# A third pair of output chunks by seven products, with tiles kept in DRAM meanwhile

## The chip, the cores and the metric

The kernel runs on one core of a Trainium2 chip. The time is that of the device in microseconds. A core has a matrix engine (TensorE, PE in the profile), a vector engine (VectorE, DVE), a scalar engine (ScalarE, ACT), GpSimd (POOL) and a queue engine (SyncE, SP). Each runs its own list of instructions in order, and waits on semaphores for the others. Sixteen DMA engines move data between DRAM and the on-chip memory (SBUF); here SP issues nearly all transfers, and GpSimd those that add to what lies in SBUF.

## What is computed

One layer of an encoder block, all in float32, 256 tokens by 2048 features:

```python
xn = rms_norm(x, norm_pre_w[l])
z = xn @ w_in[l]
u_lru, g_lru, q, k, v, g_attn, m_lru, m_attn = jnp.split(z, split_at, axis=-1)
u = centred_depthwise_conv(u_lru, conv_w[l], conv_b[l])
h = (rg_lru(u, ..., False) + rg_lru(u, ..., True))
y_a = h.astype(x.dtype) * jax.nn.silu(g_lru)
q = partial_rope(q.reshape(bsz, s, N_HEADS, HEAD_DIM), cos, sin)
k = partial_rope(k.reshape(bsz, s, N_KV_HEADS, HEAD_DIM), cos, sin)
v = v.reshape(bsz, s, N_KV_HEADS, HEAD_DIM)
y_b = windowed_gqa(q, k, v, attn_sink[l]) * jax.nn.silu(g_attn)
merged = (jax.nn.sigmoid(m_lru) * (y_a @ w_proj_a[l])
          + jax.nn.sigmoid(m_attn) * (y_b @ w_proj_b[l]))
x = x + rms_norm(merged @ w_out[l], norm_post_w[l])
```

`w_in` has 13312 columns: 2048 each for u, g_lru, q, g_attn, m_lru, m_attn, and 512 each for k and v. There are 16 heads of 128, and 4 of keys and values.

## The kernel before

**Products of float32 by three.** Every operand is split in a rounded part (`h`) and the rest (`l`), and a product is `h*h + h*l + l*h` (`mm3`, L151): three matmuls. ACT casts to `h`, DVE subtracts to get `l`.

**Steps and half steps.** The weights are read once, as rows of 1 MB (128 partitions by 2048 numbers). One row is one step of a list `steps`, and a step has two halves; the last loop of `body` (L887 to L904) walks over them. At half step `hs` it issues: the fetch of the row three steps ahead (SP, L142) into one of three buffers `raw`, whatever was put down for this half step with `at(hs, fn)` or `soon(fn, d)`, the cast and one half step later the subtraction of the half four ahead (`ahead` and `low`, L872 and L863, into one of five buffers each for `wh` and `wl`), and then the matmuls of the half. So each engine's order is written out by hand by these numbers, and the next fetch waits until DVE has subtracted both halves of an earlier row.

**Ways to make a chunk.** `add_rows` makes 512 output columns for both 128-token halves from four steps of 24 matmuls each. `add_pair` makes u and the two silu gates, features on partitions. `add_seven` (L533) makes two chunks of 512 columns at once as a 2 by 2 by 2 block product with seven block products in place of eight (`SEVEN`, L69); each takes two steps of 12 matmuls. Its left sides are blocks of the activations and four sums of blocks, e1 to e4 (`sums`, L589, which also splits them), and its right sides are weight blocks and running sums of them: those rows stay in one of two buffers `chain`, and GpSimd's DMA adds the next weight block to what lies there (L870). `spread` weaves the 14 steps of a seven among plain steps. Before the change there are two: chunks 1 and 2 of the lru merge gate (`ml`, among the gate pairs), and chunks 2 and 3 of `w_proj_a` (`pa`).

**Order.** u, ml chunk 0 and v; then the pairs for gl, ga and u with the ml seven and ml chunk 3 woven in, beside the recurrence (`lru_pair`, one every `LRU_PACE` half steps); then k; then q chunks 0 to 3 with the four chunks of the attention's merge gate (`ma`) among them as `FILL` says: q0, ma0, q1, ma1, q2, q3, ma2, ma3. Each q chunk starts four heads (`head`, L688), one every `HEADS_PACE` half steps, each a chain of PE, DVE and ACT pieces with fixed distances. After them come pa and pb, the merge, `w_out` and the tail.

**Memory.** Nearly all tiles (512 KB, that is 4 KB per partition) share `UNITS` = 31 places, and a place comes free when the last reader of its tile is done. Through the q chunks the kernel holds there the normalised x (`xn`, 8), silu(g_lru)*h = y (`sgl`, 4), the gate outputs `sga` (4), sigmoid(ml) (`tm`, 4), sigmoid(ma) (`sm`) and the attention's own tiles. The sums of x for the ml seven (`xe`) are made from half step `XE` = 36 on, at 36, 42, 48 and 54, and are dropped after it. PSUM has two double banks (`banks`) for accumulators of whole chunks, and four single ones (`bank`) for everything else.

Of the kernel before, what the change touches and what calls it, by code (L numbers as in the profile page):

```python
# [14 lines left out]
F32 = mybir.dt.float32  # L15
F32R = mybir.dt.float32r
# [4 lines left out]
P = 128  # L21
D = 2048
S = 256
# [10 lines left out]
LRU0 = 14  # L34
LRU_PACE = 18
XE = 36
XN = 15
HEAD0 = 5
HEADS_PACE = 3
FILL = ((0,), (1,), (), (2, 3))  # L40
YE = (8, 12, 18, 26)
FIRST = 8
ROWS = 10
# [31 lines left out]
def body(ctx, tc, x, xT, wall, wlru, pvec, npost, ident_d, mask_d, rope_d, out):  # L75
# [3 lines left out]
    chain = ctx.enter_context(tc.tile_pool(name="chain", bufs=CHAIN))  # L79
    ring = ctx.enter_context(tc.tile_pool(name="ring", bufs=3))  # L80
    small = ctx.enter_context(tc.tile_pool(name="small", bufs=2))
    psum = ctx.enter_context(tc.tile_pool(name="psum", bufs=4, space=PSUM))
    ctx.enter_context(tc.manual_schedule())

    def unit(name, dt=F32, shape=(P, 4, S)):
        return units.tile(list(shape), dt, tag="u", name=name)

    def bank(name, shape=(P, 2, S)):
        return psum.tile(list(shape), F32, tag="bg", name=name, bufs=4)

    def banks(name, shape=(P, 2, 2, S)):
        return psum.tile(list(shape), F32, tag="mm", name=name, bufs=2)
# [18 lines left out]
    def lag_parts(h, l, src):  # L111
        nc.scalar.copy(h, src)
        soon(lambda: nc.vector.tensor_tensor(l, src, h.bitcast(F32), ALU.subtract))

    rows_of = wall_rows()
    steps, due = [], {}
# [2 lines left out]
    def at(hs, fn):  # L119
        assert hs >= now[0], (hs, now[0])  # L120
        due.setdefault(hs, []).append(fn)
# [6 lines left out]
    def soon(fn, d=1):  # L128
        at(now[0] + d, fn)
# [57 lines left out]
    def add_rows(name, m, c, act, done, spare=False, last=False):  # L187


        got, held = [], []  # L190

        def products(t, g, h, wh, wl):
            ts = slice(t * P, (t + 1) * P)
            for j in range(2):
                k = 4 * g + 2 * h + j
                sl = slice(j * 512, (j + 1) * 512)
                a = act[k // 2][:, k % 2, :, ts]
                mm3(got[t], a[:, 0], a[:, 1], wh[:, sl], wl[:, sl], k == 0, k == KT - 1)

        def half(g, h, wh, wl):  # L200
            if g == 0 and h == 0:
                if spare:
                    got.extend(bank(f"{name}{t}", (P, 512)) for t in range(2))
                else:
                    ps = banks(name, (P, 2, 512))
                    got.extend(ps[:, t] for t in range(2))
            products(0, g, h, wh, wl)
            if last and g >= 2:
                held.append((1, g, h, wh, wl))
            else:  # L210
                products(1, g, h, wh, wl)
            if g == 3 and h == 1:
                if last:
                    done(0, got[0])
                    for a in held:
                        products(*a)
                    done(1, got[1])
                else:
                    soon(lambda: [done(t, got[t]) for t in range(2)])

        return [(("quad", m, c, g), lambda h, wh, wl, g=g: half(g, h, wh, wl), None) for g in range(4)]
# [284 lines left out]
    def gate_take(units_of, c, t, ps, scale=1.0):  # L506
        if c not in units_of:
            units_of[c] = unit(f"mg{c}", F32, (P, 2, 512))
        nc.scalar.activation(units_of[c][:, t], ps, AF.Sigmoid, scale=scale)

    def gate_evac(units_of, c, scaled=False):
        return lambda t, ps: gate_take(units_of, c, t, ps, rtok[:, t:t + 1] if scaled else 1.0)

# [72 lines left out]
                out.append((("quad", m, cols[c], 2 * r + i), lambda h, wh, wl, op=op, i=i: half(op, i, h, wh, wl), key and (name, key, i)))  # L586
        return out

    def sums(name, y):  # L589


        fm = lambda r, c, n: y[2 * c + n][:, :, r * P:(r + 1) * P]
        eight = lambda u: u.rearrange("p a (b c) -> p (a b) c", c=P)
        e, out = {}, {}

        def less(d, a, b):
            e[d] = e[b] if isinstance(b, str) else eight(unit(f"{name}{d}"))
            for n in range(2):
                f = [e[o][:, 4 * n:4 * n + 4] if isinstance(o, str) else fm(*o, n) for o in (a, b)]
                nc.vector.tensor_tensor(e[d][:, 4 * n:4 * n + 4], *f, ALU.subtract)  # L600

        def split_of(d):
            h, l = (unit(f"{name}{d}{s}", F32R, (P, 8, P)) for s in "hl")
            lag_parts(h, l, e[d])
            out[d] = (h, l)

        def when(hs):
            for (d, a, b), n in zip((("e1", (1, 0), (1, 1)), ("e2", (0, 0), "e1"), ("e4", (0, 1), "e2"), ("e3", (1, 0), (0, 0))), hs):
                at(n, lambda d=d, a=a, b=b: less(d, a, b))
                at(n + 2, lambda d=d: split_of(d))  # L610
            at(max(hs) + 4, e.clear)

        return out, when
# [10 lines left out]

        return left

    xe, xe_when = sums("xe", xt)
    xe_when([XE + n for n in (0, 6, 12, 18)])

    plain = []  # L630
# [12 lines left out]
    def add_heads(name, col, then):  # L643

        v = {}

        def evac(t, ps):
            if t == 0:
                v["t"] = unit(f"{name}t", F32, (P, 2, 512))
            nc.scalar.copy(v["t"][:, t], ps)  # L650
            if t == 1:
                soon(rotate)
                soon(flip, 3)
                for q in range(2):
                    soon(lambda q=q: part(q), 4 + q)

        def rotate():
            r = v["t"].rearrange("p t (h d) -> p t h d", h=4)
            both = small.tile([P, 2, 2, 4, ROT], F32, tag="lo", name=f"{name}r", bufs=1)
            c, m = both[:, 0], both[:, 1]  # L660
            table = lambda i, a, b: rope[:, :, i, a:b].unsqueeze(2).to_broadcast([P, 2, 4, b - a])
            half = ROT // 2
            nc.vector.tensor_tensor(m[:, :, :, 0:half], r[:, :, :, half:ROT], table(1, 0, half), ALU.mult)
            nc.vector.tensor_tensor(m[:, :, :, half:ROT], r[:, :, :, 0:half], table(1, half, ROT), ALU.mult)
            nc.vector.tensor_tensor(c, r[:, :, :, 0:ROT], table(0, 0, ROT), ALU.mult)
            nc.vector.tensor_tensor(r[:, :, :, 0:ROT], c, m, ALU.add)

        def flip():
            for q in range(2):
                v[q] = bank(f"{name}p{q}")  # L670
                for j in range(2):
                    n = 2 * q + j
                    for t in range(2):
                        nc.tensor.transpose(v[q][:, j, t * P:(t + 1) * P], v["t"][:, t, n * P:(n + 1) * P], ident)

        def part(q):
            if q == 0:
                v["h"], v["l"] = unit(f"{name}h", F32R), unit(f"{name}l", F32R)
            lag_parts(v["h"][:, 2 * q:2 * q + 2], v["l"][:, 2 * q:2 * q + 2], v[q])
            if q == 1:  # L680
                then(v["h"], v["l"])
                v.clear()

        return add_rows(f"{name}_", "w_in", col, xn, evac)
# [64 lines left out]
    def heads(g):  # L749
        def then(h, l):  # L750
            b = max(now[0] + HEAD0, ended[-1] if ended else 0)
            for j in range(4):
                head(4 * g + j, h, l, b + HEADS_PACE * j)
            ended.append(b + 4 * HEADS_PACE)
        return then
# [29 lines left out]
    def branch(name, m, y, take):  # L785
        pairs = {}

        def rows(q):
            a = pairs[q] = pair_unit(f"{name}y{q}")
            lag_parts(a[:, :, 0], a[:, :, 1], y[q // 2][:, q % 2 * 2:q % 2 * 2 + 2])  # L790

        def when(hs):
            for q in range(8):
                at(hs + q, lambda q=q: rows(q))

        def chunk(c):
            return add_rows(f"{name}{c}_", m, c * 512, pairs, lambda t, d: take(c, t, d))

        return pairs, when, chunk

    for i in range(4):
        steps += add_heads(f"q{i}", Q0 + i * 512, heads(i))
        for n in FILL[i]:
            steps += add_rows(f"ma{n}_", "w_in", MA0 + n * 512, xn, gate_evac(sm, n))
    pa, pa_when, pa_chunk = branch("pa", "w_proj_a", sgl, take_pa)
    pb, pb_when, pb_chunk = branch("pb", "w_proj_b", sga, take_pb)
    ye, ye_when = sums("ye", sgl)
    plain = [st for c in (0, 1) for st in pa_chunk(c)]
    b = 2 * len(steps)
    pb_first = pb_chunk(0)  # L810
    plain += pb_first + [st for c in (1, 2, 3) for st in pb_chunk(c)]
    pa_when(b - 4)
    ye_when([b + n for n in YE])
    steps += spread(plain, add_seven("pa", "w_proj_a", [3 * 512, 2 * 512], lefts(pa, ye), lambda t, j, d: take_pa(3 - j, t, d)), 2, 1.3)
    pb_when(2 * steps.index(pb_first[0]) - 4)
# [156 lines left out]
```

## Time and profile before

| | us |
|---|---|
| median of three runs | 904.03 (903.43 to 904.11) |
| the profiled execution | 904.01 |
| its span, first to last instruction | 902.2 |
| PE busy | 892.3 |
| DVE busy | 664.2 |
| ACT busy | 579.1 |

The mean granted TensorE clock was 0.997. In time order the stages are: u, ml0 and v to 78 us, the pairs with the recurrence and the ml seven to 403, k to 425, the q and ma chunks with the heads to 626, pa with its seven and pb to 805, and `w_out` with the tail to the end.

In the profile's rows a group reads: line of the kernel, engine, operation, tile written <- tiles read, shapes, count, then busy time and the mean of one in ns, then the time that the engine sat idle before them and what ended it. A row of a timeline begins with start and length in us. The row of a stretch gives its length and for each engine busy time and number of instructions, then the granted clock of TensorE, the share of the DMA engines and GB/s. In the list of DMAs the last number is the median time from issue to landing. `wh<-raw` is the cast of half a weight row, `wl<-raw,wh` the subtraction.

### The profile page before, as it was taken

Reading aid. Unit: us, or ns where it says so; the run is one execution under the profiler, and the core shown is the slowest. Engines: PE = TensorE matmul, PEld = TensorE weight load, DVE = VectorE, ACT = ScalarE, POOL = GpSimd, SP = SyncE. Lnnn points to the kernel's source line nnn. Section 1 sums busy time; section 2 is a strip of 40 time slices with the busy share of each in tenths; the row PEclk is TensorE's granted clock in tenths of the full one; section 3 lists DMA queues with packets and bytes.
Section 4 is the critical chain, followed back from the end, with each engine's and each line's share of the span. In section 5 each row is a group of like instructions: output and inputs, shape, how many; then the busy total and the mean of one; then the engine's idle time right before and its main releaser. Section 6 shows DMA issues by size and latency. Waiting matters only on the chain.

```text
span 902.2 us, 11861 instructions
## 1 busy us (share of the span) xinstructions
PE 892.3 (99%) x4590; PEld 763.9 (85%) x4590; DVE 664.2 (74%) x899; ACT 579.1 (64%) x807; POOL 14.6 (2%) x23
## 2 busy tenths in 40 slices
PE   9999999999999999999999999999999999999996
PEld 8888888888888888888888888888888888888885
DVE  6897989888787779696646757667888678655453
ACT  7968778786878686968455555467657555444441
POOL 0000000000000000000000000000000000000000
PEclk9999999999999999999999999999999999999998
DMA  8745686655486776545555445446757996568532
GB/s 328 259 150 216 247 278 196 229 197 232 187 237 206 234 210 199 198 168 201 184 185 173 162 144 179 147 176 242 168 205 239 243 246 196 196 218 295 189 137 94
DMA packets 29433, 184.78 MB, mean 205 GB/s; under 512 B 3264, under 2 KB 4160, under 8 KB 8768
## 3 DMA queue, kind: packets, MB, share of 16 engines
q1 hardware_dynamic: 26352, 166.08, 50.5%
q0 software_dynamic: 2304, 16.78, 10.1%
q10 hardware_dynamic: 720, 1.16, 0.4%
q8 instruction: 36, 0.59, 0.3%
q14 instruction: 21, 0.17, 0.1%
HBM read 181.90 MB, written 2.10 MB: 204 GB/s over the span
## 4 chain that ended last, share of the span: by engine, by line
PE 93%; DVE 3%; ACT 2%; DMA 1%; issue 1%; SPq 0%; DVEq 0%
PE ga L171 6%; PE gl L171 6%; PE u L171 4%; PE o L154 4%; PE o L152 4%; PE o L153 4%; PE ga L173 3%; PE gl L173 3%; PE u L173 2%; PE u_ps L354 2%; PE paq L548 2%; PE mlq L548 2%; PE pap L548 1%; PE mln L548 1%; PE pan L548 1%; PE gate L153 1%
## 5 line engine op out<-in xcount | busy, mean ns | idle before, releaser
L866 DVE TENSOR_TENSOR wl<-raw,wh 128x1024 fp32r<-128x1024 f32 x268 | 324.7, 1220 | 131.3 <-ACT wh L876 130.8
L876 ACT CAST wh<-raw 128x1024 fp32r<-128x1024 f32 x268 | 278.6, 1050 | 175.0 <-PE o L154 36.8
L876 ACT CAST wh<-chain 128x1024 fp32r<-128x1024 f32 x48 | 50.0, 1052 | 27.9 <-PE pb__6403 L154 5.0
L866 DVE TENSOR_TENSOR wl<-chain,wh 128x1024 fp32r<-128x1024 f32 x48 | 57.8, 1219 | 13.3 <-ACT wh L876 12.9
L171 PE MATMUL ga<-xn,wh 128*128 128x512 f32 x256 | 62.7, 391 | 0.0
L171 PE MATMUL gl<-xn,wh 128*128 128x512 f32 x256 | 62.7, 391 | 0.0
L171 PEld LDWEIGHTS gl<-xn,wh 128*128 128x128 f32 x256 | 47.0, 188 | 9.1
L171 PEld LDWEIGHTS ga<-xn,wh 128*128 128x128 f32 x256 | 46.9, 188 | 9.0
L152 PE MATMUL o<-wh,ms 128*128 128x512 f32 x128 | 49.9, 390 | 0.0
L154 PE MATMUL o<-wh,ms 128*128 128x512 f32 x128 | 49.8, 389 | 0.0
L153 PE MATMUL o<-wl,ms 128*128 128x512 f32 x128 | 49.8, 389 | 0.0
L171 PE MATMUL u<-xn,wh 128*128 128x512 f32 x192 | 47.4, 391 | 0.0
L171 PEld LDWEIGHTS u<-xn,wh 128*128 128x128 f32 x192 | 35.2, 188 | 6.8
L173 PEld LDWEIGHTS ga<-xn,wl 128*128 128x128 f32 x256 | 33.1, 191 | 1.4
L173 PEld LDWEIGHTS gl<-xn,wl 128*128 128x128 f32 x256 | 33.0, 191 | 1.2
L173 PE MATMUL ga<-xn,wl 128*128 128x256 f32 x256 | 33.9, 283 | 0.0
L173 PE MATMUL gl<-xn,wl 128*128 128x256 f32 x256 | 33.5, 283 | 0.0
L154 PEld LDWEIGHTS o<-wh,ms 128*128 128x128 f32 x128 | 24.0, 188 | 5.0
L153 PEld LDWEIGHTS o<-wl,ms 128*128 128x128 f32 x128 | 24.0, 188 | 5.0
L152 PEld LDWEIGHTS o<-wh,ms 128*128 128x128 f32 x128 | 24.0, 188 | 4.9
L870 POOL DMA_DIRECT2D chain<-wall_dram x16 | 14.1, 880 | 734.6 <-DVE wl L866 725.0
L173 PEld LDWEIGHTS u<-xn,wl 128*128 128x128 f32 x192 | 24.6, 191 | 0.9
(426 smaller groups left out, 2102.1 us busy)
## 6 DMA issues: line engine op xcount, KB each, us to landing
raw<-wall_dram SPq DMA_DIRECT2D x137, 1024.0 KB, 4.8
chain<-wall_dram POOLq DMA_DIRECT2D x16, 1024.0 KB, 8.1
chain<-wall_dram SPq DMA_DIRECT2D x8, 1024.0 KB, 7.0
lraw<-wlru_dram SPq DMA_DIRECT2D x8, 512.0 KB, 5.8
raw<-wall_dram SPq DMA_DIRECT2D x4, 512.0 KB, 7.2
xr<-x_dram SPq DMA_DIRECT2D x4, 512.0 KB, 9.7
raw<-wall_dram SPq DMA_DIRECT2D x4, 256.0 KB, 4.7
xT<-xT_dram SPq DMA_DIRECT2D x4, 256.0 KB, 6.5
```

The source lines that it names most:

```text
L152: nc.tensor.matmul(ps, wh, xh, start=start, stop=False)
L153: nc.tensor.matmul(ps, wh, xl, start=False, stop=False)
L154: nc.tensor.matmul(ps, wl, xh, start=False, stop=stop)
L171: nc.tensor.matmul(ps, wh[:, sl], a, start=k == 0, stop=k == KT - 1)
L173: nc.tensor.matmul(ps[:, 1], wl[:, sl], a[:, 0], start=False, stop=False)
L354: nc.tensor.matmul(ups[b // 2][:, b % 2, 0], w[:, sl], a[:, m], start=k == 0 and n == 0, stop=k == KT - 1 and n == 2)
L548: nc.tensor.matmul(d, x, y[:, sl], start=fresh and k == 0 and n == 0, stop=k == 7 and n == 2, skip_group_check=not fresh)
L866: nc.vector.tensor_tensor(wl, raws[i][:, h * 1024:(h + 1) * 1024], wh.bitcast(F32), ALU.subtract)
L870: nc.gpsimd.dma_start(raws[n], wall[rows_of[steps[n][0]]], accum_op=ALU.add)
L876: nc.scalar.copy(parts[q][0], raws[i][:, h * 1024:(h + 1) * 1024])
```

## The change

Chunks 0 and 1 of `ma` are now made by a seven, whose 14 steps are woven among the 24 steps of q0 to q3, ma2 and ma3 (`MA_SPREAD`: the first after one plain step, then one per 1.6). It needs the sums of x again. They are not made anew: when `sums` has split one, half steps later both parts are written to a DRAM pool `away` (`keep`), and read back some nine half steps before the product that takes them (`e_back`). To make room for them in the 31 places, sigmoid(ml) is written out at the end of the k chunk and read back when pa begins, and each quarter of y is written out when the recurrence has finished it and read back 14 half steps before pa begins. All these transfers are issued by SP in its order. Heads come every four half steps, not three, and the transposes of a q chunk go to one double bank, not to two single ones.

```diff
-HEADS_PACE = 3
-FILL = ((0,), (1,), (), (2, 3))
+HEADS_PACE = 4
+MA_SPREAD = (1, 1.6)
...
+    away = ctx.enter_context(tc.tile_pool(name="away", bufs=1, space=bass.MemoryType.DRAM))
...
+    def put_away(name, t):
+        d = away.tile(list(t.shape), F32, tag=name, name=f"{name}_away")
+        nc.sync.dma_start(d, t.bitcast(F32))
+        return d
+
+    def take_back(name, d, dt=F32, shape=(P, 4, S)):
+        t = unit(name, dt, shape)
+        nc.sync.dma_start(t.bitcast(F32), d)
+        return t
...
+    gone = {}
+
+    def gate_away(name, units_of, c):
+        gone[name, c] = put_away(f"{name}{c}", units_of.pop(c))
...
-    def sums(name, y):
+    def sums(name, y, keep=None):
...
+            if keep is not None:
+                soon(lambda: keep.update({d: [put_away(f"{name}{d}{s}", a) for a, s in ((h, "h"), (l, "l"))]}), 4)
...
-    xe, xe_when = sums("xe", xt)
+    kept = {}
+    xe, xe_when = sums("xe", xt, kept)
...
         def flip():
+            turned = banks(f"{name}p")
             for q in range(2):
-                v[q] = bank(f"{name}p{q}")
+                v[q] = turned[:, q]
...
+    b = 2 * len(steps)
+    for c in range(4):
+        at(b + c - 4, lambda c=c: gate_away("tm", tm, c))
+        at(LRU0 + LRU_PACE * (2 * c + 1) + 22, lambda c=c: gone.update({("ya", c): put_away(f"ya{c}", sgl[c])}))
+    plain = []
     for i in range(4):
-        steps += add_heads(f"q{i}", Q0 + i * 512, heads(i))
-        for n in FILL[i]:
-            steps += add_rows(f"ma{n}_", "w_in", MA0 + n * 512, xn, gate_evac(sm, n))
-    pa, pa_when, pa_chunk = branch("pa", "w_proj_a", sgl, take_pa)
+        plain += add_heads(f"q{i}", Q0 + i * 512, heads(i))
+    for n in (2, 3):
+        plain += add_rows(f"ma{n}_", "w_in", MA0 + n * 512, xn, gate_evac(sm, n))
+    me = {}
+    woven = add_seven("ma", "w_in", [MA0, MA0 + 512], lefts(xn, me), lambda t, j, d: gate_take(sm, j, t, d))
+    steps += spread(plain, woven, *MA_SPREAD)
+
+    def e_back(d):
+        me[d] = [take_back(f"me{d}{s}", a, F32R, (P, 8, P)) for a, s in zip(kept[d], "hl")]
+
+    for d, n in (("e1", 4), ("e4", 6), ("e3", 8), ("e2", 10)):
+        at(2 * steps.index(woven[n]) - 9, lambda d=d: e_back(d))
+    y_back = {}
+    pa, pa_when, pa_chunk = branch("pa", "w_proj_a", y_back, take_pa)
     pb, pb_when, pb_chunk = branch("pb", "w_proj_b", sga, take_pb)
-    ye, ye_when = sums("ye", sgl)
+    ye, ye_when = sums("ye", y_back)
...
     pa_when(b - 4)
+    for c in range(4):
+        at(b - 14 + c, lambda c=c: y_back.update({c: take_back(f"yb{c}", gone["ya", c])}))
+        at(b + c, lambda c=c: tm.update({c: take_back(f"tm{c}", gone["tm", c], F32, (P, 2, 512))}))
     ye_when([b + n for n in YE])
```

## The prediction

> **What bounds the kernel now.** I read the head of the page, then who TensorE waited for, then the stretches by stage, then single chunks in time.
>
> ```profile
> span 902.2 us, 11861 instructions
> PE 892.3 (99%) x4590; PEld 763.9 (85%) x4590; DVE 664.2 (74%) x899; ACT 579.1 (64%) x807; POOL 14.6 (2%) x23
> PE 93%; DVE 3%; ACT 2%; DMA 1%; issue 1%; SPq 0%; DVEq 0%
> ```
> ```profile
> PE spin L234 <- POOL eps L229: 1.0, 1, 1.0
> PE u_ps L354 <- ACT wh L105: 0.7, 1, 0.7
> ```
>
> The reader is to see that TensorE (PE) is busy for 892.3 of 902.2 us, that the chain that ended last is 93% PE, and that the whole list of PE's waits has two entries, 1.7 us together, both in the first microseconds. From there to the last chunk PE does not stop for anyone. The span is 902.2 us; the profiled execution took 904.01, so 1.81 lie around the span. That execution stands 0.02 under the median of three runs, 904.03, and I make the sum against it.
>
> ```profile
> core 0: us, PE busy (x) PEld busy (x) DVE busy (x) ACT busy (x) POOL busy (x), PEclk, DMA share, GB/s
> 78.00:180.00 102.00, 101.89 (x590) 89.94 (x589) 87.76 (x105) 80.61 (x111) 1.88 (x2) 1.00 0.68 232
> 290.00:403.00 113.00, 113.00 (x637) 99.27 (x636) 93.34 (x112) 84.96 (x114) 2.61 (x3) 1.00 0.63 198
> 425.00:640.00 215.00, 215.00 (x1067) 181.28 (x1066) 141.20 (x262) 121.79 (x194) 0.88 (x1) 1.00 0.50 175
> 640.00:700.00 60.00, 60.00 (x288) 50.29 (x288) 52.77 (x76) 39.24 (x53) 1.73 (x2) 1.00 0.68 219
> 700.00:765.00 65.00, 65.00 (x297) 53.99 (x296) 47.99 (x51) 34.62 (x37) 4.36 (x5) 1.00 0.84 226
> ```
>
> The stage that changes is that of the q chunks, the ma chunks and the heads; I take 425 to 640 for it, the first heads' half steps of pa included. There VectorE (DVE) works 141.2 of 215 us (66%), ScalarE (ACT) 121.8 (57%), the DMA engines half the time. The two stages that already hold seven-product pairs (180 to 403, and 640 to 780) run DVE at 83% (93.34 of 113) and 88% (52.77 of 60) and the DMA share up to 0.84, and PE is still full.
>
> **The change part by part.** First the matmuls. A chunk in rows has 4 steps of 24 matmuls of 512 columns, so two chunks have 192. Seven products have 14 steps of 12, which is 168. So 24 matmuls go.
>
> ```profile
> 424.96 0.39 PE L152 MATMUL q__4053<-wh,xn 128*128 128x512 f32 x1
> 433.29 0.87 PE kp L674 x8
> 447.62 0.39 PE L152 MATMUL ma__4221<-wh,xn 128*128 128x512 f32 x1
> 626.15 0.48 PE L152 MATMUL pa__5777<-wh,pay 128*128 128x512 f32 x1
> 683.94 2.72 PE paq L548 x12
> ```
>
> Chunk q0 begins at 424.96 and the next one at 447.62: 22.66 us, less 0.87 for the eight transposes put between, is 21.79 for 96 matmuls, 0.227 us each (the 0.39 of a row is one matmul's own length; they overlap). A step of seven products takes 2.72 us for 12, the same 0.227. So PE loses 24 x 0.227 = **5.44 us** of work. Heads, q transposes and all else on PE keep their count.
>
> What this costs on the other engines: 14 steps in place of 8 are 6 more, 12 halves, each with a cast on ACT and a subtraction on DVE.
>
> ```profile
> L866 DVE TENSOR_TENSOR wl<-raw,wh 128x1024 fp32r<-128x1024 f32 x66 | 80.4, 1222 | 38.9 <-ACT wh L876 38.9
> L876 ACT CAST wh<-raw 128x1024 fp32r<-128x1024 f32 x66 | 69.5, 1052 | 64.4 <-PE ma__4221 L154 10.6 <-PE q__4053 L154 9.0 <-PE q__4382 L154 8.6
> L574 DVE TENSOR_TENSOR pat<-pan,pat 128x512 f32<-128x512 f32 x1 | 0.7, 680 | 0.0
> L569 ACT COPY pat<-paq 128x512 f32<-128x512 f32 x1 | 0.6, 589 | 0.3 <-PE paq L548 0.3
> L712 ACT ACT_TABLE_LOAD x4 | 5.1, 1283 | 0.1
> ```
>
> DVE: 12 x 1.22 + 5 sums of 0.68 (L571 to L579) = 18.0, so 159.2 in about 209.6 us, 76%. ACT: 12 x 1.05 + 3 copies of 0.59 + one more pair of table loads of 1.28 (the ma sigmoids now fall in five places, not four) = 17.0, so 138.8, 66%. Both stay under the 83% and 75% of 290 to 403, so PE's work hides them, and I cost them at nothing. If that cover were gone, DVE's 18.0 would be the most that could appear.
>
> Heads three or four half steps apart: the pace is counted in half steps, and those get shorter (64 of them took 201 us, from 424.96 to the first pa matmul at 626.15, 3.14 each with the heads' matmuls among them; 76 will take some 195.8, 2.58 each). Four of the new are 10.3 us, three of the old 9.4. So a head gets about the time that it had, and the last one ends 16 half steps into the next stage (17 before). The q transposes go from two single banks of psum to one double, where accumulators change over once per chunk; a seven takes one of the four single banks through the whole stage, and a head at most three. I cost this at nothing, between a gain of 0.5 (the few short stalls now beside the transposes) and a loss of 0.5.
>
> Now SP's queue and the DMAs. Added are 16 writes of 512 KB (ml gates, y, and eight parts of the x sums) and 16 reads, 16.8 MB, and 6 more weight steps. The trace shows no write of that size, so I bound it:
>
> ```profile
> raw<-wall_dram SPq DMA_DIRECT2D x137, 1024.0 KB, 4.8
> chain<-wall_dram POOLq DMA_DIRECT2D x16, 1024.0 KB, 8.1
> chain<-wall_dram SPq DMA_DIRECT2D x8, 1024.0 KB, 7.0
> out_dram<-yw SPq DMA_DIRECT2D x4, 256.0 KB, 2.1
> GB/s 328 259 150 216 247 278 196 229 197 232 187 237 206 234 210 199 198 168 201 184 185 173 162 144 179 147 176 242 168 205 239 243 246 196 196 218 295 189 137 94
> ```
>
> A chain load is mostly issued right behind a raw load and lands 2.2 us later than one alone (7.0 against 4.8); at the fastest slice, 328 GB/s, 1.05 MB take 3.2 us. So what a transfer ahead costs the one behind it is 2.2 to 3.2 us per MB; I take 3.2. Among the q chunks this is hidden: there are 30 plain loads, 8 accumulating ones and some 7 MB more, and the stage 700 to 765 with DMA share 0.84 shows the worst of such traffic with PE full. In it PE still had the weights in hand:
>
> ```profile
> 698.65 1.22 DVE L866 TENSOR_TENSOR wl<-raw,wh 128x1024 fp32r<-128x1024 f32 x1
> 702.82 0.39 PE L152 MATMUL pb__6403<-wh,pby 128*128 128x512 f32 x1
> SPq L142 <- DVE wl L866: 669.3, 120, 12.6
> SPq L406 <- PE mlq L548: 3.8, 1, 3.8
> ```
>
> Counting halves in order, that subtraction (ends 699.87) feeds the half at 702.82: 2.95 us of lead, the shortest of that stage. Of the added waits, what is queued behind each on SP is the next weight fetch; but SP stands idle for 5.6 us per fetch anyway (669.3 in 120), waiting for the raw buffer. The writes come two or three half steps after their data, so they are ready about when SP gets there; the reads need a free place among the 31 units, and a load has already waited 3.8 us once for one (L406) with no stop on PE. Between 0 and 3.8 per read group, I take 0.
>
> The one place without cover is earlier, where the x sums are made and first written out (half steps 42 to 60, about 120 to 175 us):
>
> ```profile
> L113 DVE TENSOR_TENSOR xee2l<-xee,xee2h x1: 1220/1220/1220, 137.7 to 137.7; 128x1024 fp32r<-128x1024 f32 x1
> 155.83 1.22 DVE L113 TENSOR_TENSOR xee4l<-xee,xee4h 128x1024 fp32r<-128x1024 f32 x1
> 156.96 1.22 DVE L866 TENSOR_TENSOR wl<-raw,wh 128x1024 fp32r<-128x1024 f32 x1
> 159.42 1.22 DVE L866 TENSOR_TENSOR wl<-raw,wh 128x1024 fp32r<-128x1024 f32 x1
> ...
> 162.29 1.21 DVE L866 TENSOR_TENSOR wl<-raw,wh 128x1024 fp32r<-128x1024 f32 x1
> 163.62 0.39 PE L548 MATMUL mlp<-wh,xn 128*128 128x512 f32 x1
> 153.18 1.05 ACT L876 CAST wh<-raw 128x1024 fp32r<-128x1024 f32 x1
> 159.09 2.03 ACT L876 CAST wh<-raw 128x1024 fp32r<-128x1024 f32 x2 [1.58 <-DMA raw<-wall_dram]
> ```
>
> Here DVE runs almost without a break, and the subtraction that ends at 163.50 feeds the matmul at 163.62: 0.1 us of lead. The e2 parts (1.05 MB) are ready and written at about 139 (137.7 + 1.22); e4 (ready at 157.05) and the first y, 1.57 MB, go out at about 161, behind the fetch that waits for the subtraction of 159.42. What saves it is that DVE, not the fetch, is late: the cast of 153.18 ended at 154.23 and its subtraction came at 156.96, 2.7 us later; the pair cast from 159.09 has 2.1 us (160.14 to 162.29). The e2 writes can push the fetch between by about 2 of their 3.2; e4's writes sit behind the fetch that is needed next, and the lead after 170 grows again. So 0 to 3.2 us; I take **0.3**, near the covered end. The other writes meet leads of several us.
>
> Sum: 904.01 - 5.44 + 0.3 = **898.9 us**.
>
> **The rivals.** (1) Part is given back: one 1.05 MB write goes uncovered at the leadless place, 3.2 us: 904.01 - 5.44 + 3.2 = 901.8. For it: the 0.1 us of lead. Against: the 2.1 to 2.7 us between cast and subtraction.
> (2) Slower: there the fetches fall behind both groups of writes, 2.62 MB x 3.2 = 8.4 us, and nothing covers it, because a late cast makes a late subtraction, which frees the raw buffer late: 904.01 - 5.44 + 8.4 = 907.0. It decides once the fetches there are held up by more than 7.2 us beyond the casts' cover (5.44 are gained, 1.8 are the margin below). Against: the writes come two fetches apart, and the fetch behind the cast of 159.09 is issued between them. [...]
> (3) No change: PE's busy time isn't what sets the end, some other pace is, and the 24 matmuls leave as much idle time: 904.0. For it: the weight loads (PEld) fill 85%, not 99%. Against: the 0.227 us between matmuls is the same in a chunk of rows and in a seven, and no wait is on record. [...]
>
> **How the numbers follow.** A difference of 0.2%, 1.8 us, is about what a measurement of this kernel tells from none: faster is below 902.2, slower above 905.8. Forecast (898.2 to 900.4): 0.76. Rival 1 (900.4 to 903.5): 0.13, of which 0.08 below 902.2. Rival 2: 0.06. Rival 3: 0.05. Faster 0.84, same 0.10, slower 0.06. The range goes from 898.2 (5.44 and the 0.5 of the transposes, less 0.1) to 902.2, which leaves out about 0.17.
>
> **What would show it.** Right: PE busy near 887 us with 24 matmuls fewer, waits of PE still only those of the start, the q stage some 5.4 us shorter, DVE there at 76%. Wrong: PE waits on wl, wh, gate or sc; a PE busy sum that falls while the span doesn't (rival 3); between 150 and 175 us casts that wait for raw, and gl, mlp or gate behind them (rivals 1 and 2); fetches held on SP by a write's or a read's wait among the q chunks.

## The result, and the profile after

The changed kernel takes 899.19 us (median of six runs, 898.61 to 899.94), the kernel before 904.07 in the same comparison: a ratio of 0.9947, with a 95% interval from 0.9934 to 0.9960. A second comparison on another occasion gave 899.61 against 903.78, 0.9953 (0.9940 to 0.9965). The profiled execution took 899.15, its span is 897.0. The forecast was 898.9.

The head of the page after, and who TensorE waited for:

```profile
span 897.0 us, 11941 instructions
PE 885.6 (99%) x4566; PEld 759.1 (85%) x4566; DVE 680.5 (76%) x916; ACT 596.5 (67%) x824; POOL 21.5 (2%) x31
```
```profile
PE u_ps L365 <- ACT wh L106: 1.4, 1, 1.4
PE spin L245 <- POOL eps L240: 1.0, 1, 1.0
PE gate L163 <- ACT gi L458: 0.9, 1, 0.9
```

PE has 24 instructions fewer (4566, not 4590) and is busy 6.7 us less, the span is 5.2 us shorter. Two of the three waits are those of the first microseconds, as before. The third is new: a gate matmul of the recurrence waits 0.9 us for ACT. So some of the gain was lost in a stage that the seven doesn't touch.

The stretches (length; busy time and count by engine; granted clock; DMA share; GB/s), cut where the stages lie now:

```profile
79.00:181.00 102.00, 100.95 (x586) 89.12 (x585) 86.92 (x104) 78.44 (x107) 1.87 (x2) 1.00 0.77 269
426.00:635.00 209.00, 209.00 (x1049) 177.38 (x1048) 158.72 (x287) 138.48 (x212) 7.82 (x9) 1.00 0.76 243
```

Among the q chunks DVE now works 158.72 of 209 us (76%) and ACT 138.48 (66%), the DMA share rose from 0.50 to 0.76, and PE is full without a gap. Beside the recurrence PE is busy for 100.95 of 102 us, where it was 101.89.

Where the time went shows best from the starts of the first matmuls of each stage in the timelines. This table is worked out from those starts, in us:

| from, to | before | after | difference |
|---|---|---|---|
| span's start to the first gl matmul | 77.35 | 77.36 | +0.01 |
| first gl to first k matmul (the recurrence beside) | 325.82 | 326.88 | +1.05 |
| first k to first q matmul | 21.79 | 21.79 | 0 |
| first q to first `w_out` matmul | 381.17 | 375.19 | -5.99 |
| first `w_out` matmul to the last | 87.71 | 87.71 | 0 |
| last matmul to the span's end | 8.39 | 8.10 | -0.30 |
| around the span | 1.81 | 2.15 | +0.34 |

The rows that bound the fourth line, of before (its first row stands in the prediction) and of after:

```profile
806.14 0.39 PE L152 MATMUL o<-wh,ms 128*128 128x512 f32 x1
```
```profile
426.03 0.39 PE L163 MATMUL q__4086<-wh,xn 128*128 128x512 f32 x1
...
801.22 0.39 PE L163 MATMUL o<-wh,ms 128*128 128x512 f32 x1
```

So two things want a reason: the 5.99, which is 0.55 more than the 5.44 of the matmuls, and the 1.05 that came in earlier. The table has one more use. In the two profiles of the changed kernel the start of the first gl matmul moved by 0.65 us (77.36 and 78.01), while the stages behind it repeat within 0.1: differences of a few tenths are read from the stages, not from the whole times.

### Where the 1.05 us came from

SP's queue of the changed kernel, then the landing times of what it issued from 160.6 to 162.5, and the landing time of the same fetch in the kernel before:

```profile
160.68 0.33 SPq L153 DMA_DIRECT2D raw<-wall_dram  x1
161.06 0.43 SPq L118 DMA_DIRECT2D ya_away<-sg  x1
161.53 0.42 SPq L118 DMA_DIRECT2D xee4h_away<-xee4h  x1
162.00 0.89 SPq L118 DMA_DIRECT2D xee4l_away<-xee4l  x1
```
```profile
raw<-wall_dram SPq DMA_DIRECT2D x1, 1024.0 KB, 6.5
ya_away<-sg SPq DMA_DIRECT2D x1, 512.0 KB, 7.4
xee4h_away<-xee4h SPq DMA_DIRECT2D x1, 512.0 KB, 8.5
xee4l_away<-xee4l SPq DMA_DIRECT2D x1, 512.0 KB, 9.1
```
```profile
raw<-wall_dram SPq DMA_DIRECT2D x1, 1024.0 KB, 4.8
```

The fetch stands ahead of three writes, and yet lands 6.5 us after its issue in place of 4.8. What hangs on it is on ACT, here with PE's next gate matmul, first of before and then of after:

```profile
166.18 2.00 ACT L876 CAST wh<-raw 128x1024 fp32r<-128x1024 f32 x2
168.08 0.47 ACT L446 ACTIVATE gr<-gate,pv 128x256 f32<-128x256 f32 x1
168.45 0.47 ACT L447 ACTIVATE gi<-gate,pv 128x256 f32<-128x256 f32 x1
```
```profile
168.97 0.39 PE L152 MATMUL gate<-uh,lwh 128*128 128x256 f32 x1
```
```profile
167.22 2.00 ACT L914 CAST wh<-raw 128x1024 fp32r<-128x1024 f32 x2 [0.93 <-DMA raw<-wall_dram]
169.12 0.46 ACT L457 ACTIVATE gr<-gate,pv 128x256 f32<-128x256 f32 x1
169.49 0.46 ACT L458 ACTIVATE gi<-gate,pv 128x256 f32<-128x256 f32 x1
```
```profile
168.78 0.28 PE L165 MATMUL gate<-uh,lwl 128*128 128x256 f32 x1
170.00 0.39 PE L163 MATMUL gate<-uh,lwh 128*128 128x256 f32 x1 [0.95 <-ACT gi L458]
```

The reader is to see a chain through an engine's order. The casts wait for the fetch and run 1.04 us later (167.22 for 166.18). The sigmoids that read the gates' psum banks stand behind them in ACT's list, though they need nothing of that fetch. PE's next gate matmuls need those banks, and PE waits 0.95 us. Before, this place already had no time to spare: the gate matmul of 168.97 starts 0.05 us after the sigmoid that ends at 168.92. After, it starts at 170.00, again 0.05 after its sigmoid (169.95). The weights themselves were not late for PE: counted in order, the two subtractions of that row start at 170.39 and 171.52, as before (170.38 and 171.51), and end 6.4 to 6.6 us ahead of the matmuls that read them.

### The profile page after: what moved, and what is told of

The parts are those of the page before. It is cut to its first block, busy times and chain, and to the rows that moved or that the text cites. A ratio compares the mean times of both kernels' runs of the same rounds, so it can differ in the third digit from the quotient of the medians.

```text
span 897.0 us, 11941 instructions
## 1 busy us (share of the span) xinstructions
PE 885.6 (99%) x4566; PEld 759.1 (85%) x4566; DVE 680.5 (76%) x916; ACT 596.5 (67%) x824; POOL 21.5 (2%) x31
## 4 chain that ended last, share of the span: by engine, by line
PE 92%; ACT 2%; DVE 2%; DMA 2%; issue 1%; SPq 0%; DVEq 0%
PE ga L182 6%; PE gl L182 6%; PE u L182 4%; PE o L165 4%; PE o L164 4%; PE o L163 4%; PE ga L184 3%; PE gl L184 3%; PE u L184 2%; PE u_ps L365 2%; PE maq L564 2%; PE mlq L564 2%; PE paq L564 2%; DMA raw<-wall_dram 1%; PE man L564 1%; PE mln L564 1%
## 5 line engine op out<-in xcount | busy, mean ns | idle before, releaser
L904 DVE TENSOR_TENSOR wl<-raw,wh 128x1024 fp32r<-128x1024 f32 x256 | 309.9, 1220 | 106.0 <-ACT wh L914 105.2
L914 ACT CAST wh<-raw 128x1024 fp32r<-128x1024 f32 x256 | 266.0, 1051 | 165.4 <-PE o L165 36.8
L914 ACT CAST wh<-chain 128x1024 fp32r<-128x1024 f32 x72 | 75.0, 1051 | 39.7 <-PE pb__6724 L165 5.0
L904 DVE TENSOR_TENSOR wl<-chain,wh 128x1024 fp32r<-128x1024 f32 x72 | 86.9, 1220 | 16.2 <-ACT wh L914 15.4
L908 POOL DMA_DIRECT2D chain<-wall_dram x24 | 21.0, 877 | 722.7 <-DVE wl L904 711.0
```

The costliest lines, as they stand in the source:

```text
L904: nc.vector.tensor_tensor(wl, raws[i][:, h * 1024:(h + 1) * 1024], wh.bitcast(F32), ALU.subtract)
L908: nc.gpsimd.dma_start(raws[n], wall[rows_of[steps[n][0]]], accum_op=ALU.add)
L914: nc.scalar.copy(parts[q][0], raws[i][:, h * 1024:(h + 1) * 1024])
```

## The experiments

Eight runs follow, seven of them of kernels with an edit. The theory: PE's count of matmuls makes the gain, and the writes at 161 us cost the 1 us. The rivals: the new order, pace and banks make the gain; the 1 us is something else.

### The changed kernel once more

> The changed kernel again, beside the others on one chip. Expected as measured: about 899.2 us, span near 897.0, one new wait of PE of some 0.9 us (a gate matmul near 170 us, behind ACT's sigmoids).

It took 899.61 us (five runs), span 897.6, with the same wait of 0.9 us at the gate. The recurrence's stage was 326.81 us, the stretch from q to `w_out` 375.19, both within 0.1 of the first profile; the 0.6 us of the span lie in its start.

### The two chunks in rows again, all transfers kept

```diff
-HEADS_PACE = 4
+HEADS_PACE = 3
...
+    b = len(steps)
     for i in range(4):
-        plain += add_heads(f"q{i}", Q0 + i * 512, heads(i))
-    for n in (2, 3):
-        plain += add_rows(f"ma{n}_", "w_in", MA0 + n * 512, xn, gate_evac(sm, n))
+        steps += add_heads(f"q{i}", Q0 + i * 512, heads(i))
+        for n in ((0,), (1,), (), (2, 3))[i]:
+            steps += add_rows(f"ma{n}_", "w_in", MA0 + n * 512, xn, gate_evac(sm, n))
...
-    woven = add_seven("ma", "w_in", [MA0, MA0 + 512], lefts(xn, me), lambda t, j, d: gate_take(sm, j, t, d))
-    steps += spread(plain, woven, *MA_SPREAD)
...
-    for d, n in (("e1", 4), ("e4", 6), ("e3", 8), ("e2", 10)):
-        at(2 * steps.index(woven[n]) - 9, lambda d=d: e_back(d))
+    for d, n in (("e1", 11), ("e4", 16), ("e3", 21), ("e2", 27)):
+        at(2 * (b + n) - 9, lambda d=d: e_back(d))
```

> The changed kernel with ma chunks 0 and 1 made in rows again (192 matmuls in place of 168), in the old order and with heads every three half steps; all writes to DRAM and reads back stay, though the sums read back feed nothing. Theory (PE's count of matmuls sets the time, the writes beside the recurrence cost about 1.1 us): some 1 us slower than the kernel before, 904.9 to 905.5, PE's wait at the gate near 170 us still there. Rival (the gain comes from the new order, pace and banks and not from the count; the transfers are free): not slower than the kernel before, 903.5 to 904.3, no wait at the gate.

It took 904.76 us against 903.78: a ratio of 1.0011 (1.0002 to 1.0020). The theory had asked for 904.9 to 905.5, so the time lies 0.14 under its range. The difference of 0.98 is the 1 us that it asked for, and the sign is the theory's: without the seven, the change is slower. PE's waits:

```profile
PE spin L245 <- POOL eps L240: 1.0, 1, 1.0
PE gate L163 <- ACT gi L458: 0.9, 1, 0.9
PE u_ps L365 <- ACT wh L106: 0.2, 1, 0.2
```

The wait at the gate is there. The recurrence's stage is 327.23 us, 0.35 longer than the changed kernel's. The matmul starts show where: a matmul of the ml seven at 208.2 us starts right behind the subtraction that it reads, 0.05 us after it, and some 0.4 us are lost there. In the kernel before the same matmul had 1.5 us in hand, in the changed kernel 0.3. The three fetches that the changed kernel issues from 166.5 to 172.8 us land after 6.9, 8.6 and 7.5 us, those of the kernel before after 4.7, 4.9 and 5.8; the subtraction starts 2.26 us later than before (207.07 for 204.81), the matmul only 1.04. So the late fetches eat up the lead of a second place, which the changed kernel just clears.

```profile
206.96 1.22 DVE L902 TENSOR_TENSOR wl<-chain,wh 128x1024 fp32r<-128x1024 f32 x1
...
208.23 0.50 PE L564 MATMUL mlq<-wl,xee1h 128*128 128x512 f32 x1
```

And the stretch from q to `w_out`:

```profile
425.80 0.39 PE L163 MATMUL q__4085<-wh,xn 128*128 128x512 f32 x1
...
806.98 0.39 PE L163 MATMUL o<-wh,ms 128*128 128x512 f32 x1
```

It is 381.17 us, as in the kernel before. So the reads back, at the places that they have here, the late writes and the q transposes in a double bank cost PE nothing there, and the whole of the 5.99 belongs to the seven, with its order of the chunks, and the heads' pace. This run undoes these together; the pace alone is the fifth experiment.

### The early writes put off

```diff
+LATER = {"e1": 40, "e2": 36, "e4": 44, "e3": 40}
...
-... for a, s in ((h, "h"), (l, "l"))]}), 4)
+... for a, s in ((h, "h"), (l, "l"))]}), LATER[d])
...
-        at(LRU0 + LRU_PACE * (2 * c + 1) + 22, lambda c=c: gone.update(...))
+        at(max(98, LRU0 + LRU_PACE * (2 * c + 1) + 22), lambda c=c: gone.update(...))
```

> The changed kernel with the writes of the x sums put off by 32 to 40 half steps (half steps 78 to 96) and the first y's write to 98, where PE has its weights 4 us or more ahead. Theory (the writes near 161 us share the DMA engines with the weight fetch, its cast comes late, the sigmoids and the gate matmul behind it): the fetch issued near 160.7 lands by 165.6 again, PE's wait at the gate goes, span 895.7 to 896.3, time 1 us under the changed kernel, 897.9 to 898.4. Rival (the 1 us is not the writes' doing): wait and span stay, 897.0, time 899.2.

It took 897.95 us (897.84 to 898.19), 0.9936 of the kernel before (0.9923 to 0.9950), span 896.0. PE's waits:

```profile
PE spin L246 <- POOL eps L241: 1.0, 1, 1.0
PE u_ps L366 <- ACT wh L107: 0.7, 1, 0.7
```

The wait at the gate is gone, the fetch issued at 160.77 lands after 4.8 us again, and the recurrence's stage is 325.81 us, the 325.82 of before. Nothing else moved (375.19 from q to `w_out`). So it was the writes. Their new place is not as free as the expectation has it: at 253 us a half has only 0.05 us of lead, in the kernel before too, but the writes were issued at 213 to 217 and from 258 us on, beside it.

### The writes on GpSimd's queue

```diff
     def put_away(name, t):
...
-        nc.sync.dma_start(d, t.bitcast(F32))
+        nc.gpsimd.dma_start(d, t.bitcast(F32))
```

> The changed kernel with all its writes to DRAM issued by GpSimd, not SP. If the writes hurt by sharing the DMA engines: the fetch issued near 160.7 still lands after 166.5, PE still waits at the gate 0.5 us or more. If they hurt by standing in SP's queue: the fetch lands by 165.6, no wait at the gate, span near 896.0. A price of its own could come in: accumulating loads behind a waiting write on GpSimd's queue.

One execution: 901.07 us, span 899.2. Away from SP's queue the writes hurt more, not less. The fetch of that place lands 7.6 us after its issue, and PE:

```profile
PE gate L163 <- ACT gi L458: 2.0, 1, 2.0
PE spin L245 <- POOL eps L240: 1.0, 1, 1.0
```

That speaks for the DMA engines (from 160.7 to 167.2 us their share is 0.77 in the changed kernel, 0.42 in the kernel before) and against SP's order as the cause of the first delay. GpSimd issued the three writes at 159.38, 159.92 and 160.46, two ahead of the fetch at 160.24 and one behind it, so this run changed their time a little as well as their queue. The stage grew by 2.6 us over the changed kernel's (329.50 for 326.88), though the wait grew only by 1.1. The stretches around it hold the rest:

```profile
168.00:170.60 2.60, 0.62 (x6) 0.42 (x4) 2.60 (x4) 2.60 (x5) 0.53 (x1) 1.00 1.03 364
170.60:172.00 1.40, 1.33 (x7) 1.34 (x8) 1.40 (x2) 1.26 (x4) 0.00 (x0) 0.62 1.03 424
172.00:174.60 2.60, 2.60 (x8) 2.06 (x8) 0.90 (x2) 1.05 (x2) 0.00 (x0) 0.55 1.00 397
174.60:180.00 5.40, 5.40 (x33) 4.74 (x32) 3.71 (x5) 5.15 (x12) 0.00 (x0) 1.00 0.95 354
```

The granted clock (the last number but two) is 0.62 and then 0.55 for 4 us after PE's pause, and 1.00 again from 174.6. The DMA engines are full all the while (1.03, 1.00).

### Heads every three half steps

```diff
-HEADS_PACE = 4
+HEADS_PACE = 3
```

> The changed kernel with heads every three half steps again. Theory (at four, a head's last products and the next head's transposes always fall in the same half step, so PE is broken off 40 times between the first q matmul and the first w_out matmul in place of 47, worth 0.55 us): that stretch grows from 375.2 to about 375.7 us, no wait of PE in it. Rival (the pace of four is needed so that DVE keeps up with the seven): PE waits on sc, pt or wl there, the stretch is over 377.

One execution: 899.47 us. Between q and `w_out` PE waits for nothing, and the stretch is 375.58 us:

```profile
425.87 0.39 PE L163 MATMUL q__4086<-wh,xn 128*128 128x512 f32 x1
...
801.45 0.39 PE L163 MATMUL o<-wh,ms 128*128 128x512 f32 x1
```

That is 0.39 longer than with four. The theory had asked for 0.5, from 47 places where small matmuls break off the rows; there are 46, in place of 40 with four, which makes 0.07 us each. The pace isn't needed for the seven, and it is worth 0.4 us by itself. The count of places fits the theory's reason, that a head's last products and the next head's transposes fall in the same half step; what one such place costs was not measured apart.

### The q transposes in single banks

```diff
         def flip():
-            turned = banks(f"{name}p")
             for q in range(2):
-                v[q] = turned[:, q]
+                v[q] = bank(f"{name}p{q}")
```

> The changed kernel with the q transposes in two single banks of psum again, beside the seven that holds one. By the prediction's cost of nothing, between -0.5 and 0.5: the stretch from the first q to the first w_out matmul stays within 375.2 and 375.7, no wait of PE over 0.5 us. Rival (the double bank is needed): PE waits at the transposes for a bank, about 1 us for each of four q chunks, the stretch is over 378.

One execution: 898.31 us, 0.84 under the changed kernel's profiled execution, of which 0.74 is an earlier start of the first gl matmul (76.62 us). From q to `w_out` it is 375.19 us, the same as in the changed kernel, and PE has no wait there. The double bank makes no difference to the time.

### The early writes made twice

```diff
         nc.sync.dma_start(d, t.bitcast(F32))
+        if name[:2] == "xe" or name == "ya0":
+            twice = away.tile(list(t.shape), F32, tag=f"{name}_2", name=f"{name}_2")
+            nc.sync.dma_start(twice, t.bitcast(F32))
         return d
```

> The changed kernel with each of the eight writes of the x sums, and the first y's, made twice (to a second place in DRAM). If they hurt by sharing the DMA engines with the fetch just ahead of them: that fetch (near 160.7) lands at 168 or later in place of 167.2, the gate waits 1.7 to 3 us, and as a wait of 2.0 us was followed by some 3.4 us of a granted clock near 0.55 in the run with writes on GpSimd, another 1.5 us follow: span 898.5 to 900.5. If they hurt only what stands behind them in SP's queue: the fetch near 160.7 lands as before, the wait stays 0.9, span within 0.4 of 897.0.

One execution: 904.16 us, span 901.9, above what either had forecast. Each was wrong in part: the fetch ahead and the gate's wait stayed as the second theory said, and the span did not. The fetch ahead of the writes and PE's waits:

```profile
raw<-wall_dram SPq DMA_DIRECT2D x1, 1024.0 KB, 6.4
```
```profile
PE gl L187 <- DVE wl L907: 1.4, 1, 1.4
PE mlq L567 <- DVE wl L907: 1.1, 2, 0.8
PE u L185 <- ACT wh L917: 0.6, 1, 0.6
PE gl L185 <- ACT wh L917: 0.3, 1, 0.3
```

The fetch ahead lands after 6.4 us, no later than with single writes, and the wait at the gate is again 0.9. So here the writes behind that fetch cost it about 1.6 us, three of them or six. The rest of the writes is paid by the fetches after them: the three issued near 166.4, 168.7 and 172.7 land after 12.1, 12.3 and 10.8 us, in the changed kernel after 6.9, 8.6 and 7.5. Those use up PE's lead, and from 190 to 214 us PE waits on weights five times, 3.4 us in all. The stage is 331.97 us, 5.1 longer than the changed kernel's for 4.7 MB more to write. The granted clock is 1.00 there, from 185 to 222 us; what the expectation takes from the run on GpSimd's queue as some 3.4 us near 0.55 is, by that run's rows, 1.40 us at 0.62 and 2.60 at 0.55. The list of waits falls 1.7 us short of the 5.1, and the starts of the matmuls show why: against the changed kernel's they fall back at the same five places by 4.9 us, and by 0.2 more at 189 us. Matmuls overlap (one of 0.39 us starts every 0.227), so the time from the end of one to the start of the next, which the list counts, is less than what a stop costs.

### Only the three writes at 161 us put off

```diff
+LATER = {"e1": 4, "e2": 4, "e4": 44, "e3": 4}
```

(with the other lines of the third experiment, so the write of the second quarter of y also moves, from half step 90 to 98)

> Only the writes near 161 us (the e4 parts and the first y) are put off, those of e1, e2 and e3 stand where the change has them. Theory: all of the 1 us hangs on these three writes: no wait at the gate, span 895.7 to 896.3, 897.9 to 898.4 us. Rival (the writes add up over the stage): half of it stays, a wait of 0.3 to 0.9 us, 898.6 to 899.2.

It took 897.74 us (897.45 to 898.26), 0.9932 of the kernel before (0.9916 to 0.9949); span 895.3, of which 0.66 against the changed kernel is again an earlier start. PE's list of waits has one line:

```profile
PE spin L246 <- POOL eps L241: 1.0, 1, 1.0
```

That is a wait at the kernel's start; the gate's is gone. The recurrence's stage is 325.84 us. All of the 1 us hung on the e4 parts and the first y. The writes of e1, e2 and e3 are covered where they stand. This kernel and that of the third experiment are the fastest of the study; between them no difference is shown.

## Why the prediction was right, step by step

**The matmuls.** 24 fewer at 0.227 us, 5.44. The stretch from q to `w_out` fell by 5.99, of which 0.39 goes with the pace of the heads. That leaves 5.60. Of the 0.16 above 5.44, about 0.07 would be one place fewer where small matmuls break off the rows (46 with the pace of three, 47 before); the rest was not traced. With rows in place of the seven and the old pace the stretch is 381.17 again, to the hundredth.

**Casts, subtractions and sums of the seven hidden.** Right: DVE 159.2 and ACT 138.8 us were forecast, 158.72 and 138.48 measured, and PE has no wait in the stage.

**Pace and banks at nothing, between -0.5 and 0.5.** The sign of the pace was open; it is a gain of 0.39. Flips in a double bank: 0.

**Transfers among the q chunks at nothing.** Right, and shown by the run with rows: 381.17 with all of them, 381.17 without. SP did wait for places, in one case 5.8 us, longer than the 3.8 that the prediction allowed, and it cost nothing:

```profile
SPq L123 <- PE ma__5636 L165: 8.2, 2, 5.8
SPq L123 <- PE sc L165: 0.8, 2, 0.7
```

**The place without cover.** Here the size was off: 0.3 taken, within 0 to 3.2, and 1.05 measured. The place and its time were right, the path was not. The prediction held that the e4 writes "sit behind the fetch that is needed next" and so could not hurt it; that fetch landed 1.7 us late. And it looked for the loss in the weights' lead, where that row had over 5 us to spare; the loss came by the sigmoids that stand behind the row's casts on ACT, which had none. Of the e2 writes, which the prediction feared most, nothing was seen on PE.

Three of its readings there don't hold. It paired casts with the wrong subtractions: counted in order, the cast of 153.18 belongs to the subtraction of 162.29 and that of 159.09 to the one of 166.37, so the cover was 8.1 and 6.2 us, not 2.7 and 2.1. The place near 163 was not the only one with little lead: at 253 us a half had 0.05 us already, at 207 another had 1.5, and the latter is the one that the late fetches nearly used up. And in the stage from 700 to 765 the shortest lead is 2.3 us, at 764.4, not 2.95.

**Rivals.** Part given back (901.8): a third of it came true. Slower (907.0): its mechanism, fetches behind the writes until PE waits on weights, did not act in the changed kernel, but did when the writes were doubled, and took the whole gain (904.16). No change (904.0): excluded. At the same pace of the heads the stretch is 381.17 us with rows and 375.58 with the seven, 5.59 less for 24 matmuls, though the weight loads fill 85% of the span in the kernel before and in the changed one.

**Ends.** The sum of the parts is 904.01 - 5.99 + 1.05 + 0.01 - 0.30 + 0.34 = 899.12, and 899.15 was measured (the rest is rounding). The last two, the tail and the time around the span, nearly cancel. The prediction left both out; the row kernel has 1.8 around its span with all the DRAM tiles, so these tiles are not the reason. It stays open.

**The sum.** That 899.15 came so close to 898.9 is luck in part: the stage of the q chunks gave 0.55 more than the 5.44, the place without cover took 0.75 more than the 0.3, and these two nearly cancel.

## What to carry to other kernels

When the bounding engine has no waits, count what leaves its list, and then look for the places in the whole kernel where another engine has no lead left: here casts that came 1.04 us late cost the stage 1.05, by sigmoids that only stand behind them in ACT's order. A transfer that nobody waits for still needs a place in time; moving three writes of 0.5 MB by 40 to 44 half steps gave back 1 of the 6 us.

## What the runs showed of the hardware

A load was slowed by transfers issued after it: 4.8 us alone, 6.5 with three writes issued 0.4 to 1.3 us later on the same queue, and 6.4 with six. The next load, issued 5.8 us after it, landed after 4.8 us without the writes, 6.9 behind three and 12.1 behind six.

In the run with the writes on GpSimd's queue, a pause of PE of 2.0 us (168.6 to 170.7) was followed by a granted clock of 0.62 and 0.55 for some 4 us; a pause of 0.95 in the changed kernel left it at 1.00. The stage grew by 2.6 us and the wait by 1.1; that the 1.5 between them goes with the lower clock is the author's estimate, from one run.
